# Gaps of 32 to 128 bytes in SBUF: other start addresses, modulo 256, for streamed weights and transposed tokens, phase by phase

## The chip, the cores and the metric

The kernel runs on one core of a Trainium2 chip. The engines that matter are TensorE (PE, with its weight loads listed apart as PEld), VectorE (DVE), ScalarE (ACT), GpSimd (POOL) and the queue of SyncE (SP), which issues the weight loads from HBM. The on-chip memory is SBUF, with 128 partitions; an address in this document is a byte offset inside a partition. The metric is the device time of one execution in microseconds; before the change the median of three runs was 3052.27 us (3051.3 to 3055.29).

## The reference

256 tokens of 1024 numbers, all in float32, pass through two blocks. Cut to its frame:

```python
def reference(x, ...):
    x = first_block(x, ...)     # 4 layers: retention, conformer convolution, short convolution, retention;
                                # each followed by an MLP with relu(.)**2, RMS norms around both
    return second_block(x, ...) # 2 layers, below

def second_block(x, ...):
    for i in range(2):
        x = _layer_norm(a * x + MACARON_W * _swiglu(x, ffn_w1[i, 0], ffn_w3[i, 0], ffn_w2[i, 0]), ...)
        mix = token_mixing(x, ...)   # RWKV-7, gated linear attention, gated delta rule, gates, w_branch, w_o
        x = _layer_norm(a * x + mix, ...)
        x = _layer_norm(a * x + MACARON_W * _swiglu(x, ffn_w1[i, 1], ffn_w3[i, 1], ffn_w2[i, 1]), ...)
        ple = jax.nn.sigmoid(x @ ple_w_gate[i]) * (p[i] @ ple_w_proj[i])
        x = _layer_norm(a * x + ple, ...)
    return x
```

Nearly all arithmetic is products of the 256 tokens with weight matrices that are each used once.

## The kernel before

**Two halves of tokens.** The tokens are handled as two halves of 128. A generator for each half yields the name of the weight unit that it wants next; `drive` hands units out, the second half some units behind the first.

**Units.** A unit is 128 x 1024 numbers of weights. `load_unit` lets SP load it into a buffer `raw` or `rawx`. `split_unit` turns it into two float32r tiles: ACT rounds it into `wh` (or `whx`), and DVE subtracts that from the original into `whl` (or `whxl`). `raw` and `wh`, `whl` are pools that live all through the program; `rawx`, `whx`, `whxl` belong to the pool of a phase. Which of the two kinds a unit gets depends on which buffer is free; within a phase the two alternate irregularly.

**Tokens.** `split` does the same to transposed tokens: `t2h` from ACT and `t2l` from DVE, each 128 x 4 x 128, in the 2 KB slots (`s2`) of the phase's pool.

**Products.** `mm3` issues three matmuls of 512 columns for each product: the tokens are the stationary operand (loaded into the array by an own weight load), the weights are the moving one: `wh` with `t2h`, `whl` with `t2h`, `wh` with `t2l`. A unit therefore gives 6 matmuls for each half of the tokens. All pieces of a weight tile begin at multiples of 2048 bytes from its start, all pieces of a token tile at multiples of 512 bytes, so the remainder modulo 256 of a tile's start is that of all its 512-column operands.

**Phases.** `phase` closes the pool of the last phase and opens a new one; what is allocated first lies lowest. The program has six: the first block (kind 1), then A, M, A, M, A. M is token mixing; it has no `rawx` and `whx`. A holds the SwiGLU layers and the PLE product (`ple_in` loads its input `p` over POOL's DMA queue). In an A phase the first 20 slots of 2 KB come first, then smaller tiles, then `rawx`, `whx` and `whxl`.

**Order.** The order of each engine's instructions is that of the program text as `drive` walks it. Buffers come free by semaphores.

Where the tiles begin, as the built programs place them, modulo 256:

| phase | `wh`, `whl` | `t2h`, `t2l` | `whx`, `whxl` | tokens minus `wh` | tokens minus `whx` |
|---|---|---|---|---|---|
| 1, first block | 192 | 192 | 128 | 0 | 64 |
| 2, A | 192 | 192 | 192 | 0 | 0 |
| 3 and 5, M | 192 | 0, 64, 128 or 192, tile by tile | none | 64, 128, 192 or 0 | none |
| 4, A | 192 | 192 | 192 | 0 | 0 |
| 6, A | 192 | 192 | 192 | 0 | 0 |

Of the kernel before, what the change touches and what calls it, by code (L numbers as in the profile page):

```python
# [19 lines left out]
# (lag of the second half in units, splits ahead, loads ahead)  # L20
PACE = {"1": (4, 2, 8), "A": (4, 2, 8), "M": (0, 3, 6), "B": (2, 1, 6), "P": (6, 1, 8)}
# taps of the conformer's convolution that go to TensorE
# [3 lines left out]
# 2 KB slots, 1 KB slots  # L26
RM = (42, 20)
RINGS = {"1": (30, 6), "A": (20, 6), "M": RM}
SIDE_1 = 1.6
# [9 lines left out]
# sets of columns of w_in, a bank each; rwkv's low ranks come with the gated delta rule's a, b and GLA's low rank  # L39
# [11 lines left out]
class Builder:  # L51
    def __init__(s, ctx, tc, io):
        s.ctx, s.tc, s.nc, s.io = ctx, tc, tc.nc, io
        s.pin = tc.keep_in_program_order
        s.kind = None
        eng = s.nc.tensor
        m0, t0 = eng.matmul, eng.transpose
        def mmp(out, a, b, **k):
            r = m0(out, a, b, **k)  # L59
            n = math.prod(b.shape[1:])  # L60
            K = b.shape[0]
            f = b.dtype == F32R
            s.clock += (0.000417 * n if f else 0.001668 * max(n, 0.96 * math.prod(a.shape[1:])) * (0.75 if K == 64 else 0.6 if K == 32 else 1))
            return s.pin(r) if s.kind in PINK else r
        def trp(*a, **k):
            r = t0(*a, **k)  # L66
            s.clock += 0.107
            return s.pin(r) if s.kind in PINK else r
        s.clock = 0.0
        eng.matmul, eng.transpose = mmp, trp  # L70
        pool = lambda name, bufs, **k: ctx.enter_context(tc.tile_pool(name=name, bufs=bufs, **k))
        s.const = pool("const", 1)
        s.raw = pool("raw", RAWP)
        s.wsp = pool("wsp", WHP)
        s.vec = pool("vec", 4)
        s.st = pool("st", 8)
        s.ps = pool("ps", 1, space=PSUM)
        s.turn = False
        s.stack = None
        s.plan, s.width, s.segs = [], {}, []  # L80
        s.rawq, s.whq = ["raw"] * RAWP, ["wh"] * WHP
        s.slot, s.r, s.w, s.sh = {}, {}, {}, {}
        s.loaded = s.split_to = 0
        s.loaded_par = None
        nc = s.nc
        s.ident = s.const.tile([128, 128], F32, name="ident")
        make_identity(nc, s.ident)
        s.nhalf = s.const.tile([128, 1], F32, name="nhalf")
        nc.vector.memset(s.nhalf, -0.5)

    # ---- phases: what fills the on-chip memory
    def phase(s, kind, what):
        if s.stack is not None:
            s.stack.close()
        s.kind = kind
        s.stack = s.ctx.enter_context(ExitStack())
        s.pool = s.stack.enter_context(s.tc.tile_pool(name=f"ph{len(s.slot)}", bufs=1))
        s.rings = RINGS[kind]
        s.rawq = [t for t in s.rawq if t == "raw"]
        s.whq = [t for t in s.whq if t == "wh"]  # L100
        s.extra = EXTRA[kind]
        s.rawq += ["rawx"] * s.extra[0]
        s.whq += ["whx"] * s.extra[1]
        if kind == "M":
            s.mix_load(what)
            s.mix_params()

    # ---- tiles
# [11 lines left out]
    def any(s, tag, shape):  # L120
        """outside the projections all four banks serve alike"""
        if s.kind == "M":
            s.turn = not s.turn
            tag = "mm" if s.turn else "tp"
        return s.bank(tag, 2, shape)
# [18 lines left out]
    def rows(s, keep, name, *vecs):  # L144
        """vectors of 128 n entries as n rows each of one tile"""
        n = sum(v.shape[0] for v in vecs)
        t = s.const.tile([n, 128], F32, tag="p " + name, name=name) if keep else s.B2((n, 128), name)
        o = 0
        for v in vecs:
            s.pin(s.nc.gpsimd.dma_start(t[o:o + v.shape[0]], v))  # L150
            o += v.shape[0]
        return t

    def columns(s, name, *rows):
        """those rows as columns"""
        n = sum(r.shape[0] for r in rows)
        t = (s.pool if s.kind == "1" else s.const).tile([128, n], F32, tag="p " + name, name=name)
        tp = s.tpb((128, n))
        o = 0
        for r in rows:  # L160
            k = r.shape[0]
            s.nc.tensor.transpose(tp[:, o:o + k], r, s.ident[0:k, 0:k])
            o += k
        s.nc.vector.tensor_copy(t, tp)
        return t

    # ---- weight stream
# [9 lines left out]

    def tile_of(s, tag, dt, low=""):
        p, n = {"raw": (s.raw, RAWP), "wh": (s.wsp, WHP), "rawx": (s.pool, s.extra[0]), "whx": (s.pool, s.extra[1])}[tag]
        return p.tile([128, 1024], dt, tag=tag + low, bufs=n, name=tag + low)  # L180
# [11 lines left out]
    def split_unit(s, i, early):  # L192
        """the weights as a float32r tile and the float32r rest"""
# [25 lines left out]
    def side_step(s, wait=True):  # L219
        """one step of the mixing that is next in turn, has what it needs and whose last step is LATENCY past"""  # L220
# [21 lines left out]
    def side_run(s):  # L242
        """what goes beside half a unit"""
# [11 lines left out]
    def fill(s, u, ahead, load, stop):  # L255
        """loads and splits that run ahead of unit u; what is for another phase takes no slot of this one's"""
# [48 lines left out]
    # ---- pieces  # L305
# [34 lines left out]
    def linear(s, lhs, KT, name, n=1024, out=None):  # L340
        """units of [128 K, 1024 columns]; yields the two banks"""
        ps = out or [s.acc(), s.acc()]
        for k in range(KT):
            W = yield name
            s.mm3(lhs, k, W, [(ps[g], g * 512, 512, k == 0, k == KT - 1) for g in range(2)])
        return ps
# [6 lines left out]
    def rstd(s, v, r=None):  # L353
        """v [128, n] already holds mean square + eps"""
# [19 lines left out]
    def times(s, x, g):  # L374
        """x g, the start of rms_norm(x, g); the scale per token is left to what follows the product"""
# [6 lines left out]
    def pre_lhs(s, x, y):  # L382
        """that transposed and split, and the scale"""
# [5 lines left out]
    def post_rms(s, ps, x, g, after):  # L389
        """x + rms_norm(ps, g), and that times the vector after"""  # L390
# [14 lines left out]
    # ---- MLP  # L405
# [45 lines left out]
    # ---- retention  # L451
    def ret_consts(s):
# [9 lines left out]
        for h in range(2):  # L462
# [19 lines left out]
            # columns: cos | cos | -sin | sin  # L482
# [16 lines left out]
    def rotary(s, h, ps, rin):  # L499
        """ps: two banks of 2 heads x (t1 128 | t2 128); returns transposed [128 d, 8, 128 tok] as two tiles"""  # L500
# [84 lines left out]
    # ---- conformer conv  # L585
# [23 lines left out]
    def depthwise(s, c, raws):  # L609
        """gate and convolution of channels 256 c .. 256 c + 255, both halves; DVE and TensorE share the taps"""  # L610
# [89 lines left out]
    # ---- short conv  # L700
# [51 lines left out]
    # ---- first block  # L752
# [9 lines left out]
    def layer_vec(s, key, vec, norm=False):  # L762
        """a replicated vector, loaded by the first half that asks"""
# [38 lines left out]
    # ---- second block: SwiGLU, LayerNorm, PLE  # L802
# [47 lines left out]
    def lhs(s, src, exact):  # L850
        """transposed: as it is or split"""
# [7 lines left out]
    def post_ln(s, ps, w, x, g, b):  # L859
        """x = layer_norm(alpha * x + w * ps), taken as that of x + w / alpha * ps"""  # L860
# [42 lines left out]
    # ---- second block: token mixing  # L903
# [15 lines left out]
    def mix_load(s, i):  # L919
        """the mixers' parameters of a layer, and what is fixed"""  # L920
# [76 lines left out]
    def token_mix(s, h, lhs, i):  # L997
# [7 lines left out]
        for name, cols in SETS:  # L1005
# [7 lines left out]
            if name.startswith("gate"):  # L1013
                # sigmoid(z) = (1 + tanh(z / 2)) / 2, the last half left to the end
# [19 lines left out]
    def weave(s, main, beside):  # L1034
        """main, with a step of the other after each of its own"""
# [7 lines left out]
    def inverse(s, nb, Lq, Lx, D=None):  # L1043
        """inverses of I + L (of 1 / D + L) for strictly lower triangular 64 x 64 blocks L, two above each other in each
        of nb columns of blocks; Lq(m, q) is the transposed q-th 32 x 32 diagonal block of column m, Lx(m, e) the
        transposed lower left 32 x 32 block; returns the transposed inverses, [128, nb, 64]"""
# [67 lines left out]
    def rwkv(s, h, i, q):  # L1114
# [39 lines left out]
        # sigmoid(z) = (1 + tanh(z / 2)) / 2, the halves left to what follows  # L1154
# [22 lines left out]
        # cumulative log decay inside chunks of 64, over -exp(-1/2) / 2  # L1177
# [18 lines left out]
        # kk, 2 a * kk  # L1196
# [9 lines left out]
        # decayed: [128 channels of two heads, pair, chunk (a | r), token]  # L1206
# [22 lines left out]
        def beside():  # L1229
            """what the state will need, while the inverses are on their way"""  # L1230
# [11 lines left out]
            for c in range(2):  # L1242
# [7 lines left out]
                if c == 0:  # L1250
# [5 lines left out]
                    # values, the tokens of two heads on the partitions  # L1256
# [111 lines left out]
    def softplus(s, x, w):  # L1368
        """max(x, 0) + ln(1 + exp(-|x|))"""
# [9 lines left out]
    def gdn(s, h, i, q):  # L1379
# [29 lines left out]
        # k and q side by side, two heads a tile  # L1409
# [16 lines left out]
        # columns of ss: k 0-3, q 4-7  # L1426
# [10 lines left out]
        # ln(beta / (k.k + eps))  # L1437
# [38 lines left out]
        def beside():  # L1476
            if h:
                # keys of the first half
# [41 lines left out]
        # the second chunk of 64 after the first  # L1520
# [23 lines left out]
        # rq = (q.q + eps)^-1/2 / sqrt(dk); rms over rq * O  # L1544
# [26 lines left out]
    def gla(s, h, i, q):  # L1571
# [21 lines left out]
        for b in range(2):  # L1593
            # -(z + b)
# [6 lines left out]
        # cumulative sums of -16 log a over the half  # L1601
# [9 lines left out]
        def score(kx, qx, out, n=128, keys=(0,), queries=(0,)):  # L1611
            """scores of blocks of n keys and n queries that begin at these; out(e, bank, j-th block)"""
# [15 lines left out]
        def scaled(sz):  # L1628
            """keys of the first half of each block of 2 sz, queries of the second"""
# [203 lines left out]
```

## Time and profile before

| | |
|---|---|
| runs | 3051.3, 3052.27, 3055.29 us |
| span of the profiled execution | 3051.7 us, which lies among these runs |
| TensorE matmul (PE) | busy 2964.7 us, 97% of the span |
| weight loads (PEld) | busy 2370.0 us, 78% |
| DVE, ACT, POOL | 63%, 50%, 7% |
| DMA | 163 GB/s in the mean; most slices are at 4 to 6 tenths |
| TensorE clock granted | 0.992 in the mean |

The page lists the busy time of each engine, then the span in 40 slices, then groups of instructions by line. A matmul's row shows 0.39 us, but matmuls overlap: the next one starts about 0.23 us later. So the pace of TensorE is read from the distance of the starts in the timeline, or from the chain of work, whose pieces are these distances summed up. Addresses don't stand in a profile; those above are the program's own.

The phases can be told in the trace by their work: phase 1 ends at about 1434 us, 2 at 1627, 3 at 2012, 4 at 2430, 5 at 2816.

### The profile page before, as it was taken

Reading aid. Unit: us, or ns where it says so; the run is one execution under the profiler, and the core shown is the slowest. Engines: PE = TensorE matmul, PEld = TensorE weight load, DVE = VectorE, ACT = ScalarE, POOL = GpSimd, SP = SyncE. Lnnn points to the kernel's source line nnn. Section 1 sums busy time; section 2 is a strip of 40 time slices with the busy share of each in tenths; the row PEclk is TensorE's granted clock in tenths of the full one; section 3 lists DMA queues with packets and bytes.
Section 4 is the critical chain, followed back from the end, with each engine's and each line's share of the span. In section 5 each row is a group of like instructions: output and inputs, shape, how many; then the busy total and the mean of one; then the engine's idle time right before and its main releaser. Section 6 shows DMA issues by size and latency. Waiting matters only on the chain. (4 is left out here: it accounts for less than half of the span.)

```text
span 3051.7 us, 48503 instructions
## 1 busy us (share of the span) xinstructions
PE 2964.7 (97%) x19034; PEld 2370.0 (78%) x19034; DVE 1927.7 (63%) x3039; ACT 1521.7 (50%) x2348; POOL 216.9 (7%) x349
## 2 busy tenths in 40 slices
PE   7999998999999999999999999999999999999998
PEld 5777876787878777787887787778878788777786
DVE  6566569656665666655556857565575576567556
ACT  4345454544554544544446566544444386644443
POOL 1000025000000000200000000000020000000000
PEclk9999999999999999999999999999999999999999
DMA  7456652455566655665664333466566543335663
GB/s 236 152 175 189 183 166 83 145 181 186 178 189 183 192 162 161 202 185 177 186 186 141 92 111 107 137 202 188 181 208 188 146 147 91 106 116 170 196 188 123
DMA packets 256325, 498.52 MB, mean 163 GB/s; under 512 B 24917, under 2 KB 125473, under 8 KB 256096
## 3 DMA queue, kind: packets, MB, share of 16 engines
q1 hardware_dynamic: 247424, 470.82, 50.5%
q0 software_dynamic: 8096, 22.49, 2.6%
q8 instruction: 150, 2.46, 0.3%
q10 hardware_dynamic: 576, 2.10, 0.2%
q14 instruction: 79, 0.65, 0.1%
HBM read 494.28 MB, written 1.05 MB: 162 GB/s over the span
## 5 line engine op out<-in xcount | busy, mean ns | idle before, releaser
L59 PE MATMUL acc<-wh,t2h 128*128 128x512 f32 (+1 forms) x1736 | 714.6, 413 | 16.7 <-ACT t2h L327 16.3
L205 DVE TENSOR_TENSOR whl<-raw,wh 128x1024 fp32r<-128x1024 f32 (+1 forms) x400 | 484.5, 1214 | 344.7 <-ACT wh L204 343.7
L59 PE MATMUL acc<-whl,t2h 128*128 128x512 f32 (+1 forms) x1736 | 682.6, 394 | 0.0
L204 ACT CAST wh<-raw 128x1024 fp32r<-128x1024 f32 (+1 forms) x400 | 415.8, 1042 | 459.5 <-PE acc L59 319.3
L59 PE MATMUL acc<-wh,t2l 128*128 128x512 f32 (+1 forms) x1736 | 594.4, 394 | 1.7 <-DVE t2l L328 1.6
L59 PEld LDWEIGHTS acc<-wh,t2h 128*128 128x128 f32 x1736 | 328.1, 189 | 98.1 <-ACT t2h L327 23.7
L59 PEld LDWEIGHTS acc<-wh,t2l 128*128 128x128 f32 x1736 | 326.9, 189 | 77.8 <-DVE t2l L328 5.5
L205 DVE TENSOR_TENSOR whxl<-raw,whx 128x1024 fp32r<-128x1024 f32 x213 | 260.2, 1223 | 195.9 <-ACT whx L204 195.9
L59 PEld LDWEIGHTS acc<-whl,t2h 128*128 128x128 f32 x1736 | 328.8, 189 | 62.2 <-issue 1.8
L204 ACT CAST whx<-raw 128x1024 fp32r<-128x1024 f32 x213 | 222.6, 1049 | 213.9 <-PE mm L59 130.2
L59 PE MATMUL mm<-whx,t2h 128*128 128x512 f32 x800 | 315.2, 394 | 0.6 <-ACT t2h L327 0.6
L59 PE MATMUL mm<-whx,t2l 128*128 128x512 f32 x800 | 314.4, 393 | 0.7 <-DVE t2l L328 0.7
L59 PE MATMUL mm<-whxl,t2h 128*128 128x512 f32 x800 | 313.8, 392 | 0.0
L205 DVE TENSOR_TENSOR whl<-rawx,wh 128x1024 fp32r<-128x1024 f32 x142 | 173.7, 1225 | 140.0 <-ACT wh L204 139.7
L205 DVE TENSOR_TENSOR whxl<-rawx,whx 128x1024 fp32r<-128x1024 f32 x145 | 177.1, 1222 | 129.2 <-ACT whx L204 129.2
L59 PE MATMUL acc<-whx,t2h 128*128 128x512 f32 x632 | 256.6, 406 | 1.1 <-ACT t2h L327 1.1
L59 PE MATMUL acc<-whxl,t2h 128*128 128x512 f32 x632 | 250.5, 396 | 0.0
L204 ACT CAST whx<-rawx 128x1024 fp32r<-128x1024 f32 x145 | 151.7, 1048 | 151.4 <-PE mm L59 101.4
L204 ACT CAST wh<-rawx 128x1024 fp32r<-128x1024 f32 x142 | 149.1, 1050 | 140.8 <-PE acc L59 97.2
L59 PE MATMUL acc<-whx,t2l 128*128 128x512 f32 x632 | 201.4, 395 | 0.3 <-DVE t2l L328 0.3
L327 ACT CAST t2h<-tp 128x512 fp32r<-128x512 f32 (+1 forms) x232 | 116.1, 504 | 131.1 <-PE tp L66 103.4
L59 PEld LDWEIGHTS mm<-whx,t2l 128*128 128x128 f32 x800 | 149.9, 187 | 35.3 <-DVE t2l L328 1.1
(612 smaller groups left out, 4089.7 us busy)
## 6 DMA issues: line engine op xcount, KB each, us to landing
raw<-in_mlp_w SPq DMA_DIRECT2D x153, 512.0 KB, 3.7
raw<-in_w_in SPq DMA_DIRECT2D x128, 512.0 KB, 3.6
raw<-in_ffn_w SPq DMA_DIRECT2D x222, 256.0 KB, 3.1
rawx<-in_mlp_w SPq DMA_DIRECT2D x103, 512.0 KB, 3.7
rawx<-in_ffn_w SPq DMA_DIRECT2D x130, 256.0 KB, 3.1
raw<-in_ret_w_in SPq DMA_DIRECT2D x58, 512.0 KB, 4.3
raw<-in_ffn_w SPq DMA_DIRECT2D x50, 512.0 KB, 3.7
rawx<-in_ret_w_in SPq DMA_DIRECT2D x38, 512.0 KB, 4.4
```

The source lines that it names most:

```text
L59: r = m0(out, a, b, **k)
L204: nc.scalar.copy(wh[:, 0:n], r[:, 0:n])
L205: nc.vector.tensor_tensor(wl[:, 0:n], r[:, 0:n], wh[:, 0:n].bitcast(F32), op=ALU.subtract)
L327: nc.scalar.copy(hh, src)
```

## The change

Three gaps are put in, each as a small tile of which only one column is written (a memset on POOL).

- `gap`, 64 bytes, ahead of the pool `raw`: `raw`, `wh`, `whl`, the replicated vectors and all phase pools move up by 64 bytes.
- `gapr`, first in the pool of phases 2 (32 bytes) and 4 (128 bytes): it moves all tiles of that phase.
- `gapw`, ahead of the first `whx` in phases 4 (96 bytes) and 6 (128 bytes): it moves `whx` and `whxl` alone.

`AT` names the remainders that come out: of the token slots, and of `whx`. `wh` begins at 0.

| phase | `wh`, `whl` | `t2h`, `t2l` | `whx`, `whxl` | tokens minus `wh` | tokens minus `whx` |
|---|---|---|---|---|---|
| 1, first block | 0 | 0 | 192 | 0 | 64 |
| 2, A | 0 | 32 | 32 | 32 | 0 |
| 3 and 5, M | 0 | each 64 more than before | none | as before | none |
| 4, A | 0 | 128 | 224 | 128 | 160 |
| 6, A | 0 | 0 | 128 | 0 | 128 |

The diff without comments and the empty lines that stand in their place:

```diff
+BASE = 0
+GAP = 64
+WHX_GAP = {0: 0, 1: 0, 3: 96, 5: 128}
+AT = ((0, 192), (32, 32), None, (128, 224), None, (0, 128))
...
         s.const = pool("const", 1)
+        s.gap = pool("gap", 1)
         s.raw = pool("raw", RAWP)
...
+        s.nph, s.whx_at = -1, None
...
         make_identity(nc, s.ident)
+        s.shift(s.gap, GAP, "gap")
...
     def phase(s, kind, what):
...
+        s.nph += 1
         s.stack = s.ctx.enter_context(ExitStack())
         s.pool = s.stack.enter_context(s.tc.tile_pool(name=f"ph{len(s.slot)}", bufs=1))
+        s.at = AT[s.nph]
+        if s.at:
+            s.shift(s.pool, (s.at[0] - BASE) % 256, "gapr")
...
+    def shift(s, pool, n, name):
+        if n:
+            s.nc.gpsimd.memset(pool.tile([128, n // 4], F32, name=name)[:, 0:1], 0.0)
+
     def tile_of(s, tag, dt, low=""):
+        if tag == "whx" and s.at and len(s.at) > 1 and not low and s.whx_at is not s.at:
+            s.whx_at = s.at
+            s.shift(s.pool, WHX_GAP[s.nph], "gapw")
```

PE, ACT, DVE and SP issue the same instructions in the same order as before. POOL issues five more, all memsets. Two places of POOL's order follow, with the semaphores that a row waits for in brackets. The first is the beginning of phase 4, where the input `p` of the PLE product is loaded; `hrm` and `rstd` are reciprocal square roots. Before:

```order
L1559 TENSOR_TENSOR hrm<-hrm,nhalf 128x4 [waits DVE_49] x4
L357 TENSOR_TENSOR rstd<-var,nhalf 128x1 [waits DVE_49]
L880 DMA p<-in_p 128x256 [waits DVE_49,PE_49,DMASW1_49,Activation_49,Pool_49]
L357 TENSOR_TENSOR rstd<-var,nhalf 128x1 [waits DVE_49]
L140 DMA v<-in_ln_g 128x512 [waits DMASW5_49,DMASW2_49,DVE_49]
```

And in the change:

```order
L1578 TENSOR_TENSOR hrm<-hrm,nhalf 128x4 [waits DVE_49] x4
L376 TENSOR_TENSOR rstd<-var,nhalf 128x1 [waits DVE_49]
L192 MEMSET gapr 128x1 [waits PE_49,DVE_49,Activation_49,Pool_49]
L899 DMA p<-in_p 128x256 [waits DMASW1_49]
L192 MEMSET gapw 128x1
L376 TENSOR_TENSOR rstd<-var,nhalf 128x1 [waits DVE_49]
L152 DMA v<-in_ln_g 128x512 [waits DMASW5_49,DMASW2_49,DVE_49]
```

The wait for PE, DVE, ACT and POOL has moved from the load of `p` to the memset ahead of it.

The second place is the beginning of phase 2, after the last layer of the first block. Before:

```order
L357 TENSOR_TENSOR rstd<-msq,nhalf 128x1 [waits DVE_49,Pool_49]
L140 DMA v<-in_ln_b 128x512 [waits DMASW3_49,DVE_49]
L140 DMA v<-in_ln_b 128x512 [waits DMASW4_49,DVE_49]
L357 TENSOR_TENSOR rstd<-msq,nhalf 128x1 [waits DVE_49,Pool_49]
L357 TENSOR_TENSOR rstd<-var,nhalf 128x1 [waits DVE_49,Pool_49]
```

And in the change:

```order
L376 TENSOR_TENSOR rstd<-msq,nhalf 128x1 [waits DVE_49,Pool_49]
L192 MEMSET gapr 128x1 [waits DMAHW2_49,DMAHW3_49,DMAHW1_49,DMAHW4_49,DMAHW0_49,DMAHW5_49,DVE_49,DMAHW6_49,PE_49,DMAHW7_49,Activation_49,Pool_49]
L152 DMA v<-in_ln_b 128x512 [waits DMASW3_49,DVE_49]
L152 DMA v<-in_ln_b 128x512 [waits DMASW4_49,DVE_49]
L376 TENSOR_TENSOR rstd<-msq,nhalf 128x1 [waits DVE_49]
L376 TENSOR_TENSOR rstd<-var,nhalf 128x1 [waits DVE_49]
```

A memset that waits for everything that used the old phase's memory now stands ahead of two loads of vectors (`v`) and of a `rstd`. Of the other engines only ACT has other waits, twice: the first `t2h` of phases 3 and 5 also waits for POOL's last memset of the phase before.

## The prediction

> **What bounds the kernel.** I read the busy times first, then the stages, then the distances between matmuls. The page's first part:
>
> ```profile
> PE 2964.7 (97%) x19034; PEld 2370.0 (78%) x19034; DVE 1927.7 (63%) x3039; ACT 1521.7 (50%) x2348; POOL 216.9 (7%) x349
> ```
>
> TensorE is busy for 97% of the span and nothing else comes near. The table of busy time by stage (start to end, length, then busy time and count of PE, PEld, DVE, ACT, POOL, the granted clock, DMA share) shows the three A phases, 2, 4 and 6:
>
> ```profile
> 1434.00:1627.00 193.00, 190.30 (x865) 155.08 (x864) 105.68 (x136) 86.31 (x120) 2.62 (x5) 1.00 0.58 174
> 2012.00:2430.00 418.00, 411.28 (x1850) 334.45 (x1850) 247.43 (x318) 192.15 (x257) 23.59 (x40) 0.99 0.61 186
> 2816.00:3052.00 236.00, 220.58 (x990) 179.71 (x988) 139.52 (x181) 101.12 (x136) 10.27 (x15) 0.97 0.56 172
> ```
>
> In phases 2 and 4 PE is busy 98 to 99% of the time. DVE has 45%, 41% and 41% of the three stages free. So a matmul that starts 1 ns later each time ends the stage later by as many ns as there are matmuls: the pace of the matmul stream is the time. Hence I look at the pace and at what an address does to it. The order shows the same instructions in the same order on PE, ACT, DVE and SP; only addresses differ, and five memsets on POOL.
>
> In phase 6 the tokens and both kinds of weights begin at 192 modulo 256. The chain of work there:
>
> ```profile
> 2929.20 1.39 PE acc L59 x6
> 2930.59 8.16 PE mm L59 x36
> ```
>
> 8.16 us for 36 matmuls is **0.2267 us** each, through `wh` and `whx` in turn. In phase 1 `whx` begins at 128 and the tokens at 192. PE's timeline (start, length, instruction, count; two `t2l` matmuls can stand in one row) of a stretch that first takes a `wh` unit and then two `whx` units:
>
> ```profile
> 1091.24 0.39 PE L59 MATMUL acc<-wh,t2h 128*128 128x512 f32 x1
> ...
> 1092.62 0.39 PE L59 MATMUL acc<-whx,t2h 128*128 128x512 f32 x1
> ...
> 1094.95 0.63 PE L59 MATMUL acc<-whx,t2l 128*128 128x512 f32 x2
> 1095.42 0.39 PE L59 MATMUL acc<-whx,t2h 128*128 128x512 f32 x1
> ```
>
> From 1092.62 to 1095.42 twelve matmuls start: 2.80 / 12 = **0.2333 us** each. The `wh` unit before it, with tokens and weights both at 192, took 1.38 us for its 6, 0.230 us each: more than 0.2267, as it comes right behind other `whx` units. So the pace differs by 6.6 ns, 3%, between phases, with the same instruction and the same granted clock.
>
> Is it the address, and which? Phase 3 answers: there the weights always begin at 192, the tokens at one of four remainders.
>
> ```profile
> 1979.54 0.39 PE L59 MATMUL acc<-whl,t2h 128*128 128x512 f32 x1
> ...
> 1981.87 0.40 PE L59 MATMUL acc<-whl,t2h 128*128 128x512 f32 x1
> ...
> 1962.83 0.40 PE L59 MATMUL acc<-whl,t2h 128*128 128x512 f32 x1
> ...
> 1964.22 0.40 PE L59 MATMUL acc<-whl,t2h 128*128 128x512 f32 x1
> ...
> 2000.28 0.40 PE L59 MATMUL acc<-whl,t2h 128*128 128x512 f32 x1
> ...
> 2001.68 0.40 PE L59 MATMUL acc<-whl,t2h 128*128 128x512 f32 x1
> ```
>
> By the program's placement the tokens in the first of these stretches (10 matmuls) begin at 0, so tokens minus weights is 64: 2.33 / 10 = 0.233 us, the pace that 128 and 192 gave in phase 1, with the same difference and both addresses others. In the second (6 matmuls) the tokens are at 64, difference 128: 1.39 / 6 = 0.2317. In the third (6 matmuls) at 128, difference 192: 1.40 / 6 = 0.2333. I conclude that the **difference of the two starts modulo 256** sets the pace, that 0 is the best of the four differences seen, and that 64, 128 and 192 cost 5.0 to 6.6 ns more a matmul.
>
> **The change part by part.**
>
> *Phases 1, 3 and 5: no term.* The 64 bytes ahead of `raw` move weights and tokens alike, so the differences stay at 0 and 64 in phase 1 and at the old four values in token mixing. If single addresses count after all, this term is not 0; that is the second rival.
>
> *Phases 2, 4 and 6.* All differences were 0 and now are 32 for `wh` in phase 2, 128 for `wh` and 160 for `whx` in phase 4, 128 for `whx` in phase 6. How many matmuls that is, I read from the same stages for the tile `whx` alone, then `wh` alone (busy time and count of PE):
>
> ```profile
> 1434.00:1627.00 193.00, 89.96 (x259) 1.00 0.58 174
> 2012.00:2430.00 418.00, 194.14 (x560) 0.99 0.61 186
> 2816.00:3052.00 236.00, 99.81 (x288) 0.97 0.56 172
> ...
> 1434.00:1627.00 193.00, 94.59 (x272) 1.00 0.58 174
> 2012.00:2430.00 418.00, 200.92 (x576) 0.99 0.61 186
> 2816.00:3052.00 236.00, 111.99 (x320) 0.97 0.56 172
> ```
>
> Two of three matmuls read `wh`, the third reads `whl`, so the counts are 1.5 times these. Phase 4: 864 matmuls at difference 128, at 0.2317 - 0.2267 = 5.0 ns each, **+4.3 us**; 840 at 160, which no row shows. Its neighbours are 128 (0.2317) and 192 (0.2333), so I take 0.2325: 5.8 ns, **+4.9 us**. Phase 6: 432 at 128, **+2.2 us**. Phase 2: 408 at 32, not seen either, between 0 (0.2267) and 64 (0.2333); I take the middle, 3.3 ns, **+1.3 us**.
>
> What is unknown in these four terms is the settled pace. The stretches of phase 3 are 6 to 10 matmuls long and follow other differences, while 0.2267 is read from 36 in a row. So I bound all 2544 matmuls by the same step from both sides: 6.6 ns dearer gives +17 us, 6.6 ns cheaper -17 us. I take the values above since the nearest rows, at the very difference 128 and at 64 and 192 around it, all lie above.
>
> *Alternation.* Where units of two differences alternate, the `wh` unit above took 1.38 us instead of 6 x 0.2267 = 1.36. In phase 2 the `whx` units (388 / 6 = 65) and in phase 6 the `wh` units (480 / 6 = 80) keep difference 0 among others. 145 units at 0.02 us is 2.9 us if each follows one of the other kind; nothing if none does; I take half, **+1.5 us**.
>
> *Memsets.* A memset of one column is 0.10 us:
>
> ```profile
> 0.24 0.10 POOL L1820 MEMSET const-float32-0.0<- 128x1 f32 x1 [0.24 <-issue]
> ...
> 2012.99 0.60 POOL L880 DMA_DIRECT2D p<-in_p  x1 [2.24 <-PE tp L66]
> ...
> 2017.26 0.41 PE L66 MATMUL tp<-ident,p 128*128 128x128 f32 x2 [2.08 <-DMA p<-in_p]
> ```
>
> The memset at the start of phase 4 takes over the wait for PE that held the load of `p` until 2012.99, and PE waits 2.08 us for that load: 0.1 us of memset and about as much for one more step in the queue are on the path. The first gap stands ahead of the first vectors' load at the start of the program, which opens the path too: 0.1 us. **+0.3 us** in all. The memset of phase 2 waits for the old phase; behind it in POOL's queue stand two vectors that are needed at that phase's end, and a `rstd` that waits for DVE's work on the last product of the old phase, so later than the memset. Nothing. The `gapw` memsets wait for nothing.
>
> *ACT, DVE and DMA* work on moved tiles too:
>
> ```profile
> L204 ACT CAST whx<-raw 128x1024 fp32r<-128x1024 f32 x213 | 222.6, 1049 | 213.9 <-PE mm L59 130.2
> ...
> L204 ACT CAST wh<-rawx 128x1024 fp32r<-128x1024 f32 x142 | 149.1, 1050 | 140.8 <-PE acc L59 97.2
> ```
>
> These mix remainders 128 and 192 in and out and take 1049 and 1050 ns. I cost them at nothing; the cover is their idle time, 130 us of the cast's ahead of PE alone.
>
> **Sum:** 4.3 + 4.9 + 2.2 + 1.3 + 1.5 + 0.3 = 14.5 us on the span of 3051.7, 3066.2; the median of the runs lies 0.6 above that span, so **3067 us**.
>
> **Rivals.**
>
> *Differences not yet seen, or settled, are cheaper (faster).* The pace at 32, 128 and 160 settles below 0.2267 once a phase holds it for hundreds of matmuls. For: the three stretches are short, and the fact that one difference gives 0.2267 doesn't make that the floor. Against: the ten matmuls at 64 in phase 3 show the pace of the long stretch in phase 1, so short stretches don't mislead there. With the step of 6.6 ns downwards 2544 matmuls save 17 us: 3035. It decides from a mean pace below 0.2267 in phases 2, 4 and 6, above all in phase 4's 1704 matmuls.
>
> *The weights' own address counts (faster).* Weights at 128 are slow, weights at 192 fast: phase 1's `whx` goes from 128 to 192, and 2637 matmuls (1758 x 1.5) gain 6.6 ns, -17 us; phase 6's `whx` goes to 128, +3 us: 3038.
>
> ```profile
> 20.00:1434.00 1414.00, 615.27 (x1758) 0.99 0.56 173
> ```
>
> Against it: phase 3 has its weights at 192 and shows 0.233.
>
> *No effect on PE.* The change does not do what it says: the pace belongs to something else that differs between phases, and only the memsets remain: 3053. The Trainium skill, page "SBUF — State Buffer", section "Who interferes with whom", speaks for this one: it gives TensorE two independent read ports, one for the moving operand and one for weight loads, and says "PE and ACT never wait on anyone". By that rule no placement could slow the stream. The rows above disagree, at 0.2267 against 0.2333 us, though no row shows the mechanism.
>
> **How the numbers follow.** Forecast 0.56; unseen differences cheaper 0.17; own address 0.08; no effect 0.14; the rest, 0.05, is something unforeseen. The range takes the forecast with its upper bound (all at 6.6 ns, full alternation: 17 + 2.9 + 0.3, 3072, and 3 us for what moves in the first phase) and the lower rivals: 3035 to 3075. About 0.2%, 6 us, is what a measurement of this kernel can tell from no change. Slower by more: 0.56 and a little of the rest, less those forecasts that shrink to under 6 us: 0.55. Within: no effect, and small shifts either way, 0.20. Faster: 0.25.
>
> **What would show it.** In the chain of work of phase 4 36 matmuls in a row should take 8.3 to 8.4 us instead of 8.16; in phase 6 `wh` stretches 8.16 still and `whx` stretches more; in phase 1 the twelve `whx` matmuls should still take 2.80 us. The stages 2, 4 and 6 should be longer by about 2, 9 and 3 us, the others unchanged. Phase 4 at 8.16 or less makes the forecast wrong; a changed phase 1 makes the reasoning by differences wrong.

## The result, and the profile after

The change is slower. Four runs take 3067.22, 3068.46, 3070.16 and 3079.28 us, median 3069.31, against 3053.26 for the kernel before (four runs, 3051.3 to 3055.29). The ratio is 1.0058, 95% interval 1.0042 to 1.0074: 13 to 23 us. The profiled execution has a span of 3066.7 us, 15.0 more than before; the sum of the prediction was 14.5.

The first part of the page of the kernel after:

```profile
PE 2979.9 (97%) x19034; PEld 2370.7 (77%) x19034; DVE 1927.5 (63%) x3039; ACT 1521.3 (50%) x2348; POOL 217.2 (7%) x354
```

PE is busy 15.2 us longer with the same 19034 matmuls, the other engines work as long as before. Nothing stopped PE for long; its work became slower.

To see where, I take the same five matmuls, counted in program order, near the borders of the phases. PE's timeline of before (start, length, instruction) at the borders between phases 1 and 2, 2 and 3, and so on:

```profile
1434.07 0.39 PE L59 MATMUL acc<-whxl,t2h 128*128 128x512 f32 x1
...
1627.55 0.41 PE L59 MATMUL acc<-wh,t2h 128*128 128x312 f32 x1 [0.68 <-ACT t2h L327]
...
2013.60 0.79 PE L59 MATMUL mm<-wh,t2h 128*128 128x512 f32 x1
...
2430.82 0.41 PE L59 MATMUL acc<-wh,t2h 128*128 128x312 f32 x1 [0.24 <-ACT t2h L327]
...
2817.02 0.79 PE L59 MATMUL mm<-wh,t2h 128*128 128x512 f32 x1
```

And of after:

```profile
1434.94 0.39 PE L64 MATMUL acc<-whxl,t2h 128*128 128x512 f32 x1
...
1631.05 0.41 PE L64 MATMUL acc<-wh,t2h 128*128 128x312 f32 x1 [0.72 <-ACT t2h L346]
...
2017.43 0.79 PE L64 MATMUL mm<-wh,t2h 128*128 128x512 f32 x1
...
2443.78 0.41 PE L64 MATMUL acc<-wh,t2h 128*128 128x312 f32 x1 [0.28 <-ACT t2h L346]
...
2830.11 0.79 PE L64 MATMUL mm<-wh,t2h 128*128 128x512 f32 x1
```

The distances of these starts, and from the last one to the end of the span:

| phase | before, us | after, us | more | forecast |
|---|---|---|---|---|
| 1 | 1434.07 | 1434.94 | 0.87 | 0.1 |
| 2 | 193.48 | 196.11 | 2.63 | about 2 |
| 3 | 386.05 | 386.38 | 0.33 | 0 |
| 4 | 417.22 | 426.35 | 9.13 | about 9 |
| 5 | 386.20 | 386.33 | 0.13 | 0 |
| 6 | 234.68 | 236.59 | 1.91 | about 3 |

13.7 of the 15.0 us lie in the three A phases, two thirds of that in phase 4. There the pace shows in one stretch of 53 matmuls that ends at a transpose, the same in both programs. Before:

```profile
2125.34 0.40 PE L59 MATMUL acc<-whxl,t2h 128*128 128x512 f32 x1
...
2137.42 0.38 PE L66 MATMUL tp<-ident,glu 128*128 128x128 f32 x2
```

After:

```profile
2132.46 0.40 PE L64 MATMUL acc<-whxl,t2h 128*128 128x512 f32 x1
...
2144.84 0.38 PE L71 MATMUL tp<-ident,glu 128*128 128x128 f32 x2
```

12.08 us became 12.38: 227.9 and 233.6 ns a matmul. Phase 1, where no difference changed, kept both its paces. PE's timeline of after, a `wh` unit and then two `whx` units:

```profile
1092.12 0.40 PE L64 MATMUL acc<-wh,t2h 128*128 128x512 f32 x1
...
1093.50 0.39 PE L64 MATMUL acc<-whx,t2h 128*128 128x512 f32 x1
...
1095.83 0.63 PE L64 MATMUL acc<-whx,t2l 128*128 128x512 f32 x2
1096.30 0.39 PE L64 MATMUL acc<-whx,t2h 128*128 128x512 f32 x1
```

1.38 us for the 6 of `wh`, 2.80 us for the 12 of `whx`, both as before, though every address moved by 64 bytes. The chain of work in phase 6 shows no clean stretch of 8.16 us any more; its 36 matmuls are of both kinds:

```profile
2910.09 8.31 PE mm L64 x36
2918.40 1.38 PE acc L64 x6
...
2944.21 8.27 PE mm L64 x36
```

Over all matmuls it reads as follows. From here on "pace" is the mean distance of the starts of two matmuls that follow each other in the program, both of 512 columns of streamed weights in float32r, leaving out distances over 245 ns, which are mostly waits. "Difference" is the start of the tokens minus that of the weights, modulo 256.

| phase, tile | difference before | pace before, ns | difference after | pace after, ns |
|---|---|---|---|---|
| 1 `wh` | 0 | 229.8 | 0 | 230.0 |
| 1 `whx` | 64 | 233.3 | 64 | 233.3 |
| 2 `wh` | 0 | 227.6 | 32 | 233.3 |
| 2 `whx` | 0 | 227.6 | 0 | 229.8 |
| 4 `wh` | 0 | 227.8 | 128 | 232.9 |
| 4 `whx` | 0 | 227.8 | 160 | 233.7 |
| 6 `wh` | 0 | 227.6 | 0 | 229.3 |
| 6 `whx` | 0 | 227.6 | 128 | 231.9 |

POOL's timeline at the start of phase 4 after:

```profile
2016.29 0.10 POOL L192 MEMSET gapr<- 128x1 f32 x1 [1.72 <-DVE x L890]
2016.75 0.60 POOL L899 DMA_DIRECT2D p<-in_p  x1 [0.37 <-issue]
```

The load of `p` starts 0.68 us ahead of the phase's first matmul (2017.43) where it was 0.61, and PE waits 2.14 us for it instead of 2.08. The memset costs nothing there that could be seen.

### The profile page after: what moved, and what is told of

The parts are those of the page before. It is cut to its first block, busy times and chain, and to the rows that moved or that the text cites. A ratio compares the mean times of both kernels' runs of the same rounds, so it can differ in the third digit from the quotient of the medians.

```text
span 3066.7 us, 48512 instructions
## 1 busy us (share of the span) xinstructions
PE 2979.9 (97%) x19034; PEld 2370.7 (77%) x19034; DVE 1927.5 (63%) x3039; ACT 1521.3 (50%) x2348; POOL 217.2 (7%) x354
```

## The experiments

All kernels below are the change with other constants. The gaps are written as bytes by phase, counted from 0 (so 3 is phase 4): `TOK_GAP` stands first in the phase's pool, `WHX_GAP` ahead of its first `whx`. `GAP`, the 64 bytes at the start, stays unless said.

```diff
-AT = ((0, 192), (32, 32), None, (128, 224), None, (0, 128))
+TOK_GAP = {...}
...
-            s.shift(s.pool, (s.at[0] - BASE) % 256, "gapr")
+        s.shift(s.pool, TOK_GAP.get(s.nph, 0), "gapr")
...
-            s.shift(s.pool, WHX_GAP[s.nph], "gapw")
+            s.shift(s.pool, WHX_GAP.get(s.nph, 0), "gapw")
```

**Undo phase 4.**

```diff
+TOK_GAP = {1: 32}
+WHX_GAP = {5: 128}
```

> The change without its two gaps in phase 4 (tokens, `wh` and `whx` all at 0 there); all other gaps stay. Theory of the difference (tokens minus weights modulo 256 sets the pace): phase 4 shrinks from 426.4 us to the 417.2 us of before, the phases 2 and 6 stay at 196.1 and 236.6 us, total 3069.3 - 9.1 = 3060 us; the matmuls of phase 4 go from 232.9 (wh) and 233.7 ns (whx) back to 227.8 ns. Rival, the gaps as such (memsets and their waits at the border of the phase, other buffers): the pace of phase 4 stays above 232 ns, or the phase gets shorter at its border alone, by under 1 us: 3068 to 3069 us.

Measured: ratio to before 1.0015 (1.0006 to 1.0024), median 3057.5 us, span 3055.2. Phase 4 takes 417.67 us, with paces of 227.9 for both tiles. Phase 2 takes 196.32, phase 6 237.25. The table of busy time for 200 us of phase 4 counts the matmuls started there (behind the length: PE's busy time and count). Before, after, and this kernel:

```profile
2150.00:2350.00 200.00, 196.99 (x892) 159.90 (x891) 125.19 (x160) 94.99 (x127) 18.38 (x32) 1.00 0.62 193
```

```profile
2150.00:2350.00 200.00, 197.60 (x875) 157.28 (x874) 122.98 (x157) 92.65 (x124) 18.33 (x32) 1.00 0.62 190
```

```profile
2150.00:2350.00 200.00, 197.02 (x892) 159.86 (x891) 124.86 (x159) 95.26 (x126) 18.32 (x32) 1.00 0.63 193
```

PE is busy for 197 to 198 of the 200 us each time, at the full granted clock (the 1.00), and gets through 892, 875, 892. Phase 4 is 8.7 us shorter than in the change, and the paces alone (864 matmuls by 5.0 ns and 840 by 5.8) give 9.2; nothing is left for memsets and waits at the border. The median is 2.5 us lower than the 3060 expected. In the profiled executions phase 1 is 1.9 us shorter than in the change and phase 5 1.6, where the two programs do not differ, so an execution wanders by that much.

**All differences 0.** If the difference sets the pace, phase 1 has something to give: its `whx` had 64 all along.

```diff
+TOK_GAP = {}
+WHX_GAP = {0: 64}
```

> The gap of 64 bytes at the start stays, no gaps in phases 2, 4 and 6, and a new gap of 64 bytes ahead of `whx` in phase 1, so that tokens, `wh` and `whx` all begin at 0 in the phases 1, 2, 4 and 6. Theory of the difference: phase 1's 2640 `whx` matmuls go from 233.3 to the 227.6 ns of the A phases (-15.0 us), its 2640 `wh` matmuls from 229.9 to 227.6, as they no longer alternate with another difference (-6.1 us): phase 1 takes 1413 us instead of 1434, the total is 3052.3 - 21 + 0.3 = 3031 to 3032 us. Rival, phase 1's `whx` are slow for another reason (their place high in the memory, the traffic of that phase): they stay at 233 ns, total 3052 to 3053 us.

The same with the start gap taken out:

```diff
-GAP = 64
+GAP = 0
```

> As the kernel with all starts at 0, but without the gap of 64 bytes at the start: all starts at 192. Theory of the difference: the same pace and the same time, 3031 us, within 2 us of the kernel with all starts at 0. Rival, single addresses count beside the difference: the 5280 matmuls of phase 1 differ by up to 6.6 ns from those at 0, the two times by up to 35 us, and by 1 ns at least 8 us over all phases.

And the first of them with wider slots in token mixing:

```diff
         if kind == "M":
+            nc = s.nc
+            nc.gpsimd.memset(s.B2((128, 576), "wide")[:, 0:1], 0.0)
             s.mix_load(what)
```

> As the kernel with all starts at 0, and in the phases 3 and 5 the large slots are 2304 bytes apart instead of 2112 (one more small memset at each phase's start), so that all token tiles begin at 0 there too. Theory of the difference: the 512-column matmuls of token mixing go from a mean of 231.9 ns to at most the 229.9 ns that a difference of 0 among others gives, at best to 227.6: 2112 matmuls by 2.0 to 4.3 ns, 4 to 9 us less than with starts at 0 in the other phases alone: 3022 to 3027 us. Rival, the pace in token mixing comes from the short runs of matmuls between small ones, not from addresses: the pace and the time stay, 3031 us.

| kernel | ratio to before | median, us | span, us | phase 1, us | paces of phase 1, `wh`, `whx` |
|---|---|---|---|---|---|
| starts at 0 | 0.9960 (0.9948 to 0.9972) | 3040.6 | 3035.9 | 1418.4 | 228.1, 227.7 |
| starts at 192 | 0.9954 (0.9940 to 0.9969) | 3036.5 | 3031.9 | 1416.6 | 227.9, 227.4 |
| starts at 0, wide slots | 0.9954 (0.9942 to 0.9966) | 3039.4 | 3040.9 | 1417.8 | 228.1, 227.7 |

All three are faster than the kernel before (median 3053.5 us of 17 runs beside them). By the median they missed what was expected: 3040.6 us against 3031 to 3032, 3036.5 against the same 3031, and 3039.4 against 3022 to 3027. The count of PE in 200 us of phase 1, before and with all starts at 0:

```profile
200.00:400.00 200.00, 199.03 (x896) 160.60 (x895) 112.84 (x118) 96.06 (x119) 8.57 (x14) 1.00 0.62 186
```

```profile
200.00:400.00 200.00, 199.06 (x908) 163.15 (x907) 114.75 (x120) 97.41 (x121) 8.55 (x14) 1.00 0.63 189
```

The paces came out as expected, the time less so: 2640 matmuls by 1.7 ns and 2640 by 5.6 are 19.3 us, and phase 1 became 15.7 us shorter (1418.4 us, where 1413 were expected). Of all distances between PE's starts in phase 1, those up to 245 ns add up to 1265.1 us before and 1245.1 with starts at 0, 20.0 less; the longer ones add up to 159.7 and 163.8, 4.1 more. So the pace was gained, and longer gaps took some of it back. PE's waits in phase 1 show part of that, as those for DVE get longer. Before (us in total, times, longest):

```profile
PE acc L59 <- DVE t2l L328: 1.3, 3, 0.7
PE mm L59 <- DVE t2l L328: 1.0, 3, 0.3
PE tp L66 <- DVE cvo L653: 0.6, 1, 0.6
```

With starts at 0:

```profile
PE acc L63 <- DVE t2l L344: 1.8, 3, 0.9
...
PE mm L63 <- DVE t2l L344: 1.4, 3, 0.5
PE tp L70 <- DVE cvo L669: 1.6, 1, 1.6
```

That is 1.9 us more on these three rows (the rows of ACT's `t2h` got 0.9 us shorter). A likely reason, not shown, is that where PE hurries, what it needs from DVE at the end of a chain is not ready sooner; the rest was not traced. Starts at 0 and at 192 have paces within 0.4 ns and intervals of the ratio that overlap for the most part. Their medians lie 4.1 us apart where 2 were expected, but the six runs with starts at 192 reach from 3033.7 to 3051.3 us, the next highest being 3037.8. Single addresses, if they count, count for at most a tenth of what a difference does.

Token mixing is the miss. Its pace fell from 231.7 to 229.6 ns, worth 2.2 us in each of the two phases, but phase 3 stayed at 385.4 against 385.7 and phase 5 rose from 384.5 to 388.5, in three steps of 1.4 to 2.6 us at single places. The timed runs cannot tell this kernel from the one without wide slots. So the pace of token mixing depends on the addresses, and whether the time does stays open.

**A difference for each phase.** The tokens of each phase are moved by some bytes and `whx` moved back to 0, so that a phase has one difference throughout. Only the smaller token tiles of phase 2 (a third of its matmuls) lie behind `whx`, other than in the phases 4 and 6 and other than the sentence on A phases above says; they keep 0, so for phase 2 of the first two sweeps the table below takes the large token tiles alone.

```diff
+TOK_GAP = {0: 32, 1: 64, 3: 96, 5: 128}
+WHX_GAP = {0: 32, 1: 192, 3: 160, 5: 128}
```

> `wh` and `whx` at 0 everywhere, all tokens of a phase at one start, so that each phase has a single difference: 32 in phase 1, 64 in phase 2, 96 in phase 4, 128 in phase 6. Theory 1 (every difference other than 0 is slow by itself): the paces settle at 231.9 to 233.7 ns, as 32, 64, 128 and 160 had them among others; against the kernel with all starts at 0 (227.9 ns) 5280, 796, 1704 and 912 matmuls get about 5.5 ns dearer, 29 + 4 + 9 + 5 = 47 us: about 3085 us, phase 1 near 1446 us. Theory 2 (what costs is that units of two differences alternate; a phase that keeps one settles): 227 to 228 ns in all four phases, 3036 to 3040 us.

```diff
+TOK_GAP = {0: 160, 1: 128, 3: 192, 5: 224}
+WHX_GAP = {0: 160, 1: 128, 3: 64, 5: 32}
```

> The same with 160 in phase 1, 128 in phase 2, 192 in phase 4, 224 in phase 6. Theory 1: 232 to 234 ns in each, about 3085 us. Theory 2: 227 to 228 ns, 3036 to 3040 us. Theory 3 (how far the two starts lie apart around the ring of 256 bytes decides: 224 is 32 away, 192 is 64 away): the pace is the same for a difference and for 256 minus it, so 160 like 96, 192 like 64, 224 like 32; 128 alone has no partner.

Since 192 came out cheap, the differences were then exchanged between phases:

```diff
+TOK_GAP = {0: 192, 1: 0, 3: 224, 5: 96}
+WHX_GAP = {0: 128, 1: 0, 3: 32, 5: 160}
```

> As the sweeps before, with 192 in phase 1, 0 in phase 2, 224 in phase 4, 96 in phase 6: each difference in another phase than where it was measured. Theory (the pace belongs to the difference, wherever it stands): 192 is the cheap one among the others also in phase 1, 229.0 ns as in phase 4, so phase 1 is 1.1 ns x 5280 = 6 us longer than with all starts at 0 (1418.4), 1424 us; phase 2 at 227.9 ns, 194 us; phase 4 at 233.4 ns, 428 us; phase 6 at 234.2 ns, 240 us; total about 3056 us. Rival (each phase has its own cheap difference, by its work and its other tiles): phase 1 at 233 ns, 1446 us and more, total about 3078 us.

The first sweep was repeated, since its phase 1 had a jump (see the last section):

> The first sweep once more (32, 64, 96, 128 in phases 1, 2, 4, 6). Its phase 1 had one jump of 9.5 us at a single matmul of the convolution behind GpSimd's diagonal matrices, beside the pace. Theory 1 (the jump was that of one execution): the paces come out as before within 0.3 ns, phase 1 is 1443 us, the total about 3081 us. Rival (moving the phase by 32 bytes makes that step of GpSimd slow): phase 1 is 1452 us again, with the jump at the same matmul, total 3091 us.

| difference | pace, ns (phase, kernel) |
|---|---|
| 0 | 227.7 to 228.1 (1, 2, 4 and 6, starts at 0); 227.8 to 228.0 (2, third sweep) |
| 32 | 233.0 `wh`, 233.3 `whx` (1, first sweep, the same in its repeat); 233.3 (2, the change) |
| 64 | 233.3 (1 `whx`, before and after); 233.3 (2, first sweep and repeat) |
| 96 | 234.1 to 234.2 (4, first sweep and repeat; 6, third sweep) |
| 128 | 232.4 to 232.5 (6, first sweep and repeat); 232.9 (4 `wh`, the change); 233.1 (2, second sweep) |
| 160 | 233.4 (1, second sweep); 233.7 (4 `whx`, the change) |
| 192 | **229.0** (4, second sweep); 229.1 (1, third sweep) |
| 224 | 233.4 (6, second sweep); 233.3 (4, third sweep) |

The times were 3091.2 us (one run) and 3077.0 (the repeat, two runs; ratio to before 1.0079, 1.0050 to 1.0109) for the first sweep, 3070.5 for the second and 3059.3 for the third (one run each). A difference has its pace wherever it stands: 192 is 229.0 ns in phase 4 and 229.1 in phase 1, and phase 1 took 1424.6 us where 1424 was expected. The counts of 200 us of phase 4 at 96, 192 and 224 are:

```profile
2150.00:2350.00 200.00, 197.39 (x871) 156.96 (x870) 122.75 (x156) 91.83 (x122) 18.34 (x32) 1.00 0.63 190
```

```profile
2150.00:2350.00 200.00, 197.40 (x889) 159.64 (x889) 124.35 (x158) 93.80 (x124) 18.33 (x32) 1.00 0.63 193
```

```profile
2150.00:2350.00 200.00, 197.35 (x875) 156.52 (x874) 123.03 (x157) 92.74 (x123) 18.37 (x32) 1.00 0.62 190
```

Theory 2 (alternation alone costs) falls: phases with one difference stay slow. Theory 3 (distance around the ring) falls: 64 and 192 are 233.3 and 229.0. Theory 1 holds for all but 192. The second sweep, with 192 in phase 4, ended 14.5 us below the 3085 of theory 1; 1704 matmuls at some 4.5 ns less are about 8 us of that.

**Less than 32 bytes.** The weights are moved inside a wider tile, by floats:

```diff
+W_OFF = {0: 4, 1: 2, 3: 6, 5: 1}
...
-        return p.tile([128, 1024], dt, tag=tag + low, bufs=n, name=tag + low)
+        if tag[0] == "w":
+            o = W_OFF.get(s.nph, 0)
+            return p.tile([128, 1088], dt, tag=tag + low, bufs=n, name=tag + low)[:, o:o + 1024]
```

> All tokens at 0, all float32r weight tiles moved inside a wider tile: by 16 bytes in phase 1, 8 in phase 2, 24 in phase 4, 4 in phase 6, 0 in token mixing. Theory 1a (blocks of 32 bytes or more count): starts in one block are like a difference of 0: 227.5 to 228.2 ns in all phases, 3036 to 3040 us. Theory 1b (the exact difference counts): 232 to 234 ns, about 3085 us. Theory 1c (a row that begins inside a block touches one block more): any pace above 229 ns, the same for 4, 8, 16 and 24.

Paces: 231.5 to 231.8 ns at 16 bytes, 233.3 at 8, 234.0 at 24, 237.1 at 4; time 3076.3 us in one run. 1a falls: there is no block in which starts are alike, and 4 bytes off are the dearest of all that was tried. 1c in its form, one price for all four, falls as well. Here the weights moved and the tokens stayed, so every weight row also begins off a multiple of 32; whether the price belongs to the difference or to the weights' own start was not told apart for these small shifts.

**Which tokens?** In the A phases and phase 1 of the kernels so far a matmul's own tokens and those of the next matmul, which are loaded meanwhile, nearly always begin at the same remainder, so the two could not be told apart. Here `t2l` is moved alone, in wider slots:

```diff
+L_OFF = {3: 16, 5: 32}
...
-        ll = s.B2((128, n, 128), "t2l", F32R)
+        if s.nph in L_OFF:
+            o = L_OFF[s.nph]
+            ll = s.B2((128, 576), "t2l", F32R)[:, o:o + n * 128].rearrange("p (n t) -> p n t", n=n)
+        else:
+            ll = s.B2((128, n, 128), "t2l", F32R)
```

> All starts at 0, except that `t2l` begins at 64 in phase 4 and at 128 in phase 6. A product's six matmuls are wh t2h, whl t2h, wh t2h, whl t2h, wh t2l, wh t2l; the start-to-start time of each is read by its place 1 to 6. Theory N (the weights of a matmul meet the stationary tokens of the next one, which are loaded meanwhile): places 4 and 5 have a difference and are the dear ones, 6 is cheap. Theory O (they meet the matmul's own tokens): 5 and 6 are dear, 4 is cheap. In both the mean lies between 228 and 231 ns; a price that lasts over several matmuls can blur the places, and then what differs by over 1 ns between 4 and 6 decides.

The medians of the six places, over products that follow a `t2l` and without waits inside (32 in phase 6, 53 in phase 4; ns):

| | 1 | 2 | 3 | 4 | 5 | 6 |
|---|---|---|---|---|---|---|
| all starts at 0, phases 4 and 6 | 227 | 227 | 227 | 227 | 227 | 227 |
| `t2l` at 128, phase 6 | 227.5 | 227 | 227 | 233 | 241 | 239 |
| `t2l` at 64, phase 4 | 229 | 232 | 230 | 227 | 235 | 230 |

One such product of phase 6 in PE's timeline; the last row but one holds both `t2l` matmuls:

```profile
2882.14 0.39 PE L64 MATMUL acc<-wh,t2h 128*128 128x512 f32 x1
...
2882.82 0.40 PE L64 MATMUL acc<-whl,t2h 128*128 128x512 f32 x1
2883.05 0.64 PE L64 MATMUL acc<-wh,t2l 128*128 128x512 f32 x2
2883.53 0.40 PE L64 MATMUL mm<-whx,t2h 128*128 128x512 f32 x1
```

The first three take 0.68 us, the fourth 0.23, the two with `t2l` 0.48. By the rule set down (4 against 6) the matmul's own tokens are what the weights meet: 6 is dearer than 4 by 6 and 3 ns. But it is no clean verdict, since 4, whose own tokens are at 0, is dear too in phase 6, and places 2 and 3 in phase 4. Token mixing before, where the tokens differ from tile to tile, does not settle it: sorted by a matmul's own tokens, 0 has 230.9 ns and 64, 128 and 192 have 232.5 to 232.7; sorted by the next one's, 0, 64, 128 and 192 have 231.5, 231.7, 233.4 and 231.1, a wider spread. The price is not in the next load alone; what exactly meets what stays open.

The mean pace tells more. It was expected between 228 and 231 ns and came out at 231.4 in phase 4 and 231.8 in phase 6. Against 227.8 that is 3.6 and 4.0 ns for moving a third of the token operands, where moving all of them cost 5.5 (at 64) and 4.6 to 4.7 (at 128). So a phase's pace is not the sum of what each matmul's own difference would cost. One run took 3045.9 us, against 3054.7 for the kernel before in the same set.

## Why the prediction was right

*The pace is the time, and the difference sets it.* Right for phases whose tokens begin at one remainder. The change moved only the phases whose differences it moved; taking two gaps out of phase 4 gave its time back; and exchanging differences between phases exchanged their paces. For a single matmul among others the rule is too simple, as the run that moves `t2l` alone shows; by what mechanism the addresses meet stays open. The three A phases together grew by 13.7 us against 14.2 (the sum without the memsets). That the whole came out at 15.0 against 14.5 is in part luck: 1.3 us of it are from the phases 1, 3 and 5, where 0.1 was forecast.

*Phases 1, 3 and 5: no term.* Right on the paces. The 1.3 us that these phases gained is no more than what phases 1 and 5 wandered between two kernels that are alike there.

*Phase 4, 4.3 + 4.9 us.* Right: 5.1 ns for `wh` and 5.9 for `whx` were measured against 5.0 and 5.8, and 9.13 us against 9.2. The value for 160, taken between its neighbours 128 and 192, came out right by luck: 192, one of the two, settles at 229.0 and not at the 233.3 that a stretch of six matmuls had shown. Halfway between the settled paces of 128 and 192 (5.1 and 1.2 ns above 227.8) would have been about 3 ns, 2.2 us too little for the phase.

*Phase 2, 1.3 us for `wh` at 32.* The mis-sized term: I took the middle between 0 and 64, 3.3 ns, and 5.7 were measured, 2.3 us for 408 matmuls. There is no slope between 0 and 64; already 4 bytes off cost more than 64.

*Phase 6, 2.2 us.* A little high: 432 matmuls by 4.3 ns are 1.9 us; with the alternation that is 2.7 us by the paces, of which 1.9 reached the phase.

*Alternation, 1.5 us.* Right: 2.2 ns on 388 `whx` matmuls of phase 2 and 1.7 ns on 480 `wh` matmuls of phase 6 are 1.7 us. For the same reason one of the signs named did not come: phase 6 kept no stretch of 8.16 us, as its `wh` matmuls went from 227.6 to 229.3 ns.

*Memsets, 0.3 us.* Not to be seen at phase 4; that at the start of the program can't be told from the wandering of phase 1.

*The rivals.* "Differences not yet seen are cheaper" falls: all of 32 to 224 are dearer than 0. "The weights' own address" falls: phase 1's `whx` at 192 instead of 128 kept 233.3 ns. "No effect on PE" falls with phase 4. Beside this rival the prediction named the Trainium skill, page "SBUF — State Buffer", section "Who interferes with whom", by which PE never waits on anyone. The trace agrees in that PE waited for no other engine in these stretches. The reading by which the prediction let it speak for this rival, that no placement could slow the stream, falls: the same work at other addresses ran 2.5% slower (233.6 against 227.9 ns). No run here shows whether PE's own reads meet each other.

## What to carry to other kernels

Where PE is busy for 97% of a kernel and still not at its best, read the distance of matmul starts phase by phase; a pace that differs between phases with the same instruction and clock can come from where the operands lie. In this kernel phases in which all token and weight tiles start at the same remainder modulo 256 ran at 227 to 228 ns, those at any other difference but 192 at 231.5 to 237, and moving a third of the token operands already cost most of that; padding one phase so that all differences are 0 was worth 0.4% (0.9954 to 0.9960). Take a settled pace from dozens of matmuls in a row, not from six, and expect less back than the paces promise: 15.7 of 19.3 us here.

## What was not expected of the hardware

- One difference of the seven multiples of 32 beside 0, 192, is nearly free (229.0 ns against 232.4 to 234.2), and its mirror image 64 is not.
- Weights that start 4 bytes off cost 9.3 ns a matmul (237.1 against 227.8), more than any multiple of 32.
- In the first sweep one of GpSimd's diagonal matrices (`dg`) took as long as 30 operations of DVE beside it. Its timeline, POOL and then DVE:

```profile
510.26 13.70 POOL L661 TENSOR_SCALAR dg<-ident,cfc 128x128 f32<-128x128 f32 x3 [3.85 <-PE mm L63]
```

```profile
510.37 11.95 DVE L665 SCALAR_TENSOR_TENSOR cvo<-win,cfc,cvo 128x256 f32<-128x256 f32 x30
522.25 0.68 DVE L594 BATCH_NORM_STATS2 bn<-tp 128x6 f32<-128x512 f32 x1
```

Three of POOL's operations last 13.70 us, the first of them alone 12.54, over the very time of 30 operations of DVE, and PE waits for the result. The other 51 of this kind in this execution take 0.60 to 2.40 us: 0.60 in the median where no SCALAR_TENSOR_TENSOR of DVE runs beside them, 2.40 where five do. The bracket of PE's next row says 9.37 us:

```profile
522.85 1.65 PE L63 MATMUL mm<-win,dg 128*128 128x256 f32 x3 [9.37 <-POOL dg L661]
```

In the repeat, the same program, PE has no such wait, phase 1 takes 1441.0 us instead of 1452.3 and the span is 3074.6 instead of 3089.4. The Trainium skill, page "SBUF — State Buffer", section "Who interferes with whom", says that GpSimd and DVE share ports that one of them holds for a whole instruction. The trace agrees in that `dg` takes longer the more operations of DVE run beside it, and shows in addition that it can last over 30 of them in a row. It does not show the ports themselves, nor why this happened in one execution and not in the repeat.
